# Attention of a hybrid decoder trunk in three visits to TensorE instead of five, with a bank pair lent by the dense sums

## The chip, the cores and the metric

The kernel runs on one core of one Trainium2 chip. The metric is the device time in microseconds (us) of one execution. The engines of the core work side by side, each through its own ordered queue: TensorE (PE in the profile; its weight loads are PEld), VectorE (DVE), ScalarE (ACT), GpSimdE (POOL) and SyncE (SP), which issues the weight DMAs. TensorE writes its results to PSUM, eight banks of 512 float32 per partition; VectorE and ScalarE read them from there.

## The reference

Two layers over 256 positions of width 1024, float32. Each layer is a feed-forward step, a mixing step and a second feed-forward step, each on the RMS-normalised input and added to it:

```python
def hybrid_layer(x, ...):
    x = x + 0.5 * swiglu(rms_norm(x, ffn1_norm), ffn1_w_gate_up, ffn1_w_down)
    h = rms_norm(x, mix_norm)
    z = h @ w_in                       # 512 for pooling, 3 x 512 for q, k, v, 2048 for gates
    u, q, k, v, gl = ...
    y_pool = multiscale_pool(u, pool_w, pool_scale)    # trailing means over 2/4/8/16, minus the token, a 128x128 map per group
    q = rope(rms_norm(q.reshape(B, S, 8, 64), q_norm))
    k = rope(rms_norm(k.reshape(B, S, 8, 64), k_norm))
    y_attn = moba_attention(q, k, v)
    gates = sigmoid(gl + b_gate).reshape(B, S, 2, 1024)
    merged = gates[:, :, 0] * (y_pool @ w_branch_pool) + gates[:, :, 1] * (y_attn @ w_branch_attn)
    x = x + merged @ w_out
    return x + 0.5 * swiglu(rms_norm(x, ffn2_norm), ffn2_w_gate_up, ffn2_w_down)
```

The block-sparse attention has blocks of 256 positions, and there are 256 positions: no block lies fully in the past, and what remains is plain causal attention of 8 heads of width 64.

## The kernel before

**Dense work.** Activations lie with features on partitions. Each float32 operand is split into a high and a low part (float32r). A product of a 128x128 weight block with all 256 positions is one step of `chain` (L142): the high weights with both parts of the activations (512 columns), then the low weights with the high part (256 columns). The sum of two output blocks over eight input blocks, 16 such steps, is one `sum_pair` (L173) into a tile of two PSUM banks from the pool `pmm`, which has two such tiles. `drain` (L188) evacuates it: ScalarE copies one half (L189), VectorE adds the other (L190). Only then can the pool hand these banks to the next tile.

**Weights.** `request` (L97) issues the DMA of one unit of 16 blocks (1 MB) and splits it in two halves, each by a ScalarE copy (L122) and a VectorE subtraction (L123). The split parts have six half-unit buffers, three units. Each pair of gates requests one unit while it uses an older one.

**The mixing step** (`mix`, L575) projects q, k and v by token, turns q and k to features (`to_features`), projects the pooling input (`project_u`), and then computes the eight pairs of gate columns, f = 0 to 7: `gate(f)` is one `sum_pair`, a `request` and the drain into `gates[:, f]`; `open_gate(f)` scales on VectorE (L603) and applies Tanh on ScalarE (L606). Attention and the pooling maps are laid in between, for four pairs of heads p = 0 to 3. Queries are cut at 128: the early half (positions 0 to 127) needs 128 keys, the late half 256. They use the other four PSUM banks, the pool `pat`: first as two tiles of two banks (`flat`, each holding the scores of one pair of heads, 384 columns a head), at the end as four tiles of one bank (`half_psum(4)`, `quarter`). Before the change TensorE comes to them five times in a layer:

1. in the middle of gate 0: the scores of pairs 0 and 1 (`score(0, 1)`);
2. after gate 2: the transposes of their probabilities (`turn(0, 1)`), copied to SBUF by ScalarE (`turned`, L561);
3. in the middle of gate 3: the scores of pairs 2 and 3, then the values of pairs 0 and 1 into the free quarter of the same tiles (`second`);
4. after gate 5: the transposes of pairs 2 and 3, and the pooling maps of groups 0 and 1 (`third`);
5. after gate 6: the values of pairs 2 and 3 and the maps of groups 2 and 3 (`fourth`).

`softmax` (L531) works on one pair of heads: VectorE adds the mask in PSUM (L534), takes the maxima (L538) and scales them (L540); ScalarE takes four exponentials with their sums (L543); VectorE inverts the sums (L545) and normalises (L548). `heads_end` (L661, L662) and `map_end` (L656, L657) split the results into high and low parts in `yp`. After gate 7's sum the branch products (tile `two`) read `yp`.

**Order.** Matmuls and whatever is wrapped in `keep` stay in the order written. The other instructions of ScalarE and VectorE are ordered by a planner when the program is built, which gives each engine a fixed queue; the order of VectorE and ScalarE is therefore planned anew when the code changes.

**The feed-forward step** (`ffn`, L312) opens with two pairs whose steps are interleaved. `factor_parts`, `factor_sums` and `factor_end` make the normalising factor from the sum of squares `acc`. `more` is given for a feed-forward step that follows a mixing step; without it, and without `n0`, this branch serves only the first feed-forward step of layer 1.

Of the kernel before, what the change touches and what calls it, by code (L numbers as in the profile page):

```python
# [24 lines left out]
P = 128  # L25
# [24 lines left out]
def trunk_kernel(ctx: ExitStack, tc: tile.TileContext, x_in, w_in, pw_in, qkn_in, rope_in, mask_in, band_in, out):  # L50
# [131 lines left out]
    def pair(w, t, other=None, at=0):  # L182

        ps = sum_pair(w, other, at)
        request()
        drain(t, ps)
# [125 lines left out]
    def ffn(after, n0=0, end=False, more=None):  # L312
# [18 lines left out]
        else:  # L331
# [188 lines left out]
    def scores(qT, kT, p, sc):  # L520

        for c, qs, ks in ((slice(0, S), slice(P, S), slice(0, S)), (slice(S, 3 * P), slice(0, P), slice(0, P))):
            for h in range(2):
                hs = slice(h * DH, (h + 1) * DH)
                mm(sc[:, h, c], lhsT=qT[hs, p, qs], rhs=kT[hs, p, ks], start=True, stop=True)

    COLS = (slice(S, 3 * P), slice(0, S))

    def softmax(sc, p, pr, rq):  # L531

        dg = sc[:, :, P:3 * P].rearrange("p h (a b) -> p h a b", a=2)
        tt(dg, dg, mask.unsqueeze(1).unsqueeze(1).to_broadcast([P, 2, 2, P]), op=OP.add)  # L534
        nb = small.tile([P, 2, 2], F32, name="nb", tag="nb")
        su = small.tile([P, 2, 2], F32, name="su", tag="su")
        for t, c in enumerate(COLS):
            nc.vector.tensor_reduce(nb[:, t, :], sc[:, :, c], axis=AX.X, op=OP.max)  # L538
        rp = rq.rearrange("p (t h) -> p t h", t=2)[:, :, 2 * p:2 * p + 2]
        stt(nb, nb, -1.0, rp, op0=OP.mult, op1=OP.mult)  # L540
        for h in range(2):
            for t, c in enumerate(COLS):
                act(pr[:, h, c], sc[:, h, c], AF.Exp, scale=rp[:, t, h:h + 1], bias=nb[:, t, h:h + 1],  # L543
                    accum_out=su[:, t, h:h + 1])
        nc.vector.reciprocal(su, su)  # L545
        for t, c in enumerate(COLS):
# [3 lines left out]
    def by_key(pr, pt):  # L550

        for h in range(2):
            for o, c in enumerate((2, 0, 1)):
                j = 3 * h + o
                keep(nc.tensor.transpose(line(pt)[:, j * P:(j + 1) * P], pr[:, h, c * P:(c + 1) * P], ident))  # L555

    def line(z):
        return z.rearrange("p h s -> p (h s)")

    def to_key(pt, pT):  # L560
        act(line(pT)[:, :6 * P], line(pt)[:, :6 * P], AF.Copy)  # L561

    def values(pT, v, p, y):

        for i, t in ((0, 0), (1, 0), (1, 1)):
            for s in range(2):
                h = 2 * p + s
                c = (3 * s + i + t) * P
                mm(y[s * DH:(s + 1) * DH, i], lhsT=v[:, t, h * DH:(h + 1) * DH],
                   rhs=line(pT)[:, c:c + P], start=t == 0, stop=t == i)  # L570
# [4 lines left out]
    def mix(l, after):  # L575
# [23 lines left out]
        def gate(f, *other):  # L599
            pair(unit(), gates[:, f], *other)  # L600
# [71 lines left out]
        rest = slice(3 * P, 4 * P)  # L672
# [4 lines left out]
        ats = []  # L677

        def score(*ps):
            ats[:] = [flat() for _ in ps]  # L680
            for p, sc in zip(ps, ats):
                scores(qT, kT, p, sc)

        def turn(*ps):
            ats[:] = [flat() for _ in ps]
            for p, pt in zip(ps, ats):
                by_key(pp[:, p % 2], pt)

        def turned(*ps):
            for p, pt in zip(ps, ats):  # L690
                to_key(pt, pp[:, 2 + p % 2])

        def second():
# [263 lines left out]
```

## Time and profile before

| | |
|---|---|
| median of 3 runs | 998.58 us (998.3 to 1006.34) |
| the profiled execution | 998.18 us |
| its span, first to last instruction | 996.3 us |
| TensorE busy | 991.8 us (100%) |
| VectorE busy | 812.7 us (82%) |
| ScalarE busy | 637.3 us (64%) |
| granted TensorE clock | 1.000 |
| from HBM | 190.82 MB, 193 GB/s over the span |

Times in the profile are microseconds from the first instruction of the span, unless marked ns. A row of the timeline gives start, duration, engine, line and operation, output<-inputs and, in brackets, the engine's idle time before it with what ended it. Successive instructions overlap a little at their ends, so that a row's duration is somewhat longer than the time for which it holds its engine. A row of the chain of waits gives start, length, engine, tile and line, and the number of instructions. A row of the groups gives line, engine, operation, tiles and shapes, the count, then the sum of busy time, the mean in ns and the idle time before them. A float32 matmul that is not split appears as two instructions. Layer 1's gates begin at about 720 us, layer 0's at about 227 us.

### The profile page before, as it was taken

What the parts mean: (1) busy time and instruction counts of PE and PEld (TensorE: products, weight loads), DVE (VectorE), ACT (ScalarE), POOL (GpSimd) and SP (SyncE); (2) the same over time, 40 slices, a digit from 0 to 9 for tenths busy, and PEclk for the clock granted to TensorE, in tenths of its full rate; (3) what the DMA queues carried; (4) which work ended last, traced back from release to release, by engine and by line L of the source; (5) the groups of instructions that cost most, each with busy time, mean ns of one, the idle gap of its engine ahead of it and who ended that gap; (6) DMA issues with size and microseconds to landing.
All of it is one profiled execution on the core that took longest, in us unless ns stands there. A gap on an engine that the chain in (4) does not pass through costs nothing.

```text
span 996.3 us, 15513 instructions
## 1 busy us (share of the span) xinstructions
PE 991.8 (100%) x6059; PEld 891.3 (89%) x6059; DVE 812.7 (82%) x1227; ACT 637.3 (64%) x1028; POOL 3.5 (0%) x54
## 2 busy tenths in 40 slices
PE   9999999999999999999999999999999999999998
PEld 8898889898898989888989889888989989889887
DVE  7987786699889998886678888667998999888752
ACT  7766565657867866665566666556678668656541
POOL 1000000000000000000000000000000000000000
PEclk9999999999999999999999999999999999999999
DMA  9665566653635665656555655555545356655540
GB/s 314 242 208 209 192 245 216 214 177 113 226 127 180 234 221 186 203 204 205 184 204 178 208 206 180 207 206 191 186 152 198 110 190 232 228 203 184 211 143 27
DMA packets 30152, 192.86 MB, mean 194 GB/s; under 512 B 3360, under 2 KB 5408, under 8 KB 7552
## 3 DMA queue, kind: packets, MB, share of 16 engines
q1 hardware_dynamic: 29664, 191.18, 55.1%
q8 instruction: 47, 0.77, 0.3%
q10 hardware_dynamic: 288, 0.31, 0.1%
q0 software_dynamic: 128, 0.39, 0.1%
q14 instruction: 25, 0.20, 0.1%
HBM read 190.82 MB, written 1.05 MB: 193 GB/s over the span
## 4 chain that ended last, share of the span: by engine, by line
PE 99%; DMA 0%; ACT 0%; SPq 0%; DVE 0%; issue 0%
PE ps L80 85%; PE pt L80 6%; PE two L80 4%; PE at L80 2%; PE at L555 1%; PE pe L80 0%; DMA raw<-w 0%; PE tp L516 0%; PE ss L80 0%; ACT hi L122 0%; SPq L834 0%; DVE gx L460 0%; ACT hx L252 0%
## 5 line engine op out<-in xcount | busy, mean ns | idle before, releaser
L80 PE MATMUL ps<-hx,hi 128*128 128x512 f32 (+1 forms) x1714 | 571.9, 383 | 0.1
L123 DVE TENSOR_TENSOR lo<-raw,hi 128x1024 fp32r<-128x1024 f32 (+2 forms) x333 | 392.4, 1186 | 110.5 <-ACT hi L122 106.6
L80 PE MATMUL ps<-hx,lo 128*128 128x256 f32 x1712 | 464.3, 273 | 0.0
L122 ACT ACTIVATE hi<-raw 128x1024 fp32r<-128x1024 f32 (+2 forms) x333 | 339.0, 1028 | 177.5 <-PE ps L80 148.1
L80 PEld LDWEIGHTS ps<-hx,hi 128*128 128x128 f32 x1714 | 320.8, 188 | 57.3 <-issue 0.3
L80 PEld LDWEIGHTS ps<-hx,lo 128*128 128x128 f32 x1712 | 320.9, 188 | 0.9 <-DVE lo L123 0.2
L80 PE MATMUL ps<-ga,hi 128*128 128x512 f32 x256 | 86.9, 382 | 0.0
L80 PE MATMUL ps<-gc,hi 128*128 128x512 f32 x256 | 86.9, 382 | 0.0
L80 PE MATMUL ps<-ga,lo 128*128 128x256 f32 x256 | 69.9, 273 | 0.0
L80 PE MATMUL ps<-gc,lo 128*128 128x256 f32 x256 | 69.9, 273 | 0.0
L80 PE MATMUL ps<-gb,hi 128*128 128x512 f32 (+1 forms) x197 | 65.6, 377 | 0.0
L80 PE MATMUL pt<-hi,hx 128*128 128x512 f32 x192 | 64.5, 383 | 0.0
L80 PEld LDWEIGHTS ps<-gc,hi 128*128 128x128 f32 x256 | 48.1, 188 | 8.6
L80 PEld LDWEIGHTS ps<-ga,hi 128*128 128x128 f32 x256 | 48.1, 188 | 8.6
L80 PE MATMUL pt<-lo,hx 128*128 128x256 f32 x192 | 52.5, 273 | 0.0
L80 PE MATMUL ps<-gb,lo 128*128 128x256 f32 x192 | 52.4, 273 | 0.0
L190 DVE TENSOR_TENSOR ab<-ps,ab 128x512 f32<-128x512 f32 x56 | 38.5, 688 | 16.1 <-ACT ab L189 14.8
L80 PEld LDWEIGHTS ps<-ga,lo 128*128 128x128 f32 x256 | 48.1, 188 | 0.0
L80 PEld LDWEIGHTS ps<-gc,lo 128*128 128x128 f32 x256 | 48.1, 188 | 0.0
L397 DVE TENSOR_TENSOR lo<-raw,hi 128x1024 fp32r<-128x1024 f32 x38 | 44.7, 1217 | 0.0
L80 PE MATMUL two<-yp,hi 128*128 128x512 f32 x128 | 42.8, 382 | 0.0
L80 PE MATMUL ps<-mk,hi 128*128 128x512 f32 x128 | 42.8, 382 | 0.0
(161 smaller groups left out, 1126.2 us busy)
## 6 DMA issues: line engine op xcount, KB each, us to landing
raw<-w SPq DMA_DIRECT2D x176, 1024.0 KB, 4.9
raw<-w SPq DMA_DIRECT2D x6, 256.0 KB, 6.1
raw<-w SPq DMA_DIRECT2D x11, 128.0 KB, 3.8
raw<-w SPq DMA_DIRECT2D x2, 512.0 KB, 7.3
gx<-x SPq DMA_DIRECT2D x2, 256.0 KB, 5.3
qk<-pw SPq DMA_DIRECT2D x2, 256.0 KB, 2.7
out_dram<-gx SPq DMA_DIRECT2D x2, 256.0 KB, 2.1
out_dram<-gx SPq DMA_DIRECT2D x1, 384.0 KB, 5.8
```

Of the source, the lines that this page charges most:

```text
L80: return keep(nc.tensor.matmul(*args, **kw))
L122: put(act(hi, w, AF.Copy))
L123: put(tt(lo, w, hi.bitcast(F32), op=OP.subtract))
L190: put(tt(t, ps[:, :, 0, :], t, op=OP.add))
L397: keep(tt(lo[h], raw[:, h * HALF:(h + 1) * HALF], hi[h].bitcast(F32), op=OP.subtract))
L555: keep(nc.tensor.transpose(line(pt)[:, j * P:(j + 1) * P], pr[:, h, c * P:(c + 1) * P], ident))
```

## The change

TensorE comes to attention three times in a layer.

- `score`, in the middle of gate 0: the scores of all four pairs. The late queries' scores go to the two tiles of `pat`, two pairs in each (256 columns a head). The early queries' scores of all pairs go to a tile `low` that is taken from `pmm`, the pool of the dense sums. `largest` then makes the masked early scores in SBUF (one wide add into `pp`), masks the late ones in PSUM, and takes all maxima of the layer (three reductions, one scaling). Gate 1's sum is written into the same `low` tile.
- `softmax` is left with exponentials, inverse and normalisation, one pair after each of gates 0 to 3.
- `turn`, after a quarter of gate 5's sum: all 24 transposes, the early ones into a second `low` tile from `pmm`, the late ones into two tiles of `pat`; then one ScalarE copy of the early ones and four of the late ones. Gate 6's sum is written into that second `low` tile.
- `finish`, in the middle of gate 6: all values and all four pooling maps, into four tiles of one bank, and their drains.

The matmuls themselves keep their number and their sizes. In the first feed-forward step of layer 1 the two opening pairs are interleaved in another order, the drain of the first comes ahead of the factor, the factor's sum over partitions stands before the last eight steps of the second pair instead of behind them, and three instructions lose their `keep`.

```diff
-    def sum_pair(w, other=None, at=0):
-        ps = banks(pmm, "ps")
+    def sum_pair(w, other=None, at=0, ps=None):
+        ps = ps or banks(pmm, "ps")
...
-            for u, k0, k1 in ((0, 0, 6), (1, 0, 4), (0, 6, NK)):
+            for u, k0, k1 in ((0, 0, 6), (1, 0, 4), (0, 6, NK)) if more else ((0, 0, 7), (1, 0, 2), (0, 7, NK), (1, 2, 4)):
                 columns(ws[u], pss[u], range(k0, k1))
-            ar = factor_parts(keep)
-            drain(ts[0], pss[0], keep)
-            for _ in range(1 if more else 0):
+            if more:
+                ar = factor_parts(keep)
+                drain(ts[0], pss[0], keep)
                 more()
+            else:
+                drain(ts[0], pss[0])
+                r.append(factor_end(factor_sums(factor_parts())))
             columns(ws[1], pss[1], range(4, NK))
-            r.append(factor_end(factor_sums(ar)))
+            if more:
+                r.append(factor_end(factor_sums(ar)))
...
+    def largest(ats, low, pp, rq):
+        tt(pp[:, :, :, LOW], low, mask.unsqueeze(1).unsqueeze(1).to_broadcast([P, 4, 2, P]), op=OP.add)
+        nb = small.tile([P, 2, 8], F32, name="nb", tag="nb")
+        for i, at in enumerate(ats):
+            for p in range(2):
+                dg = at[:, :, p, P:]
+                tt(dg, dg, bc2(mask), op=OP.add)
+            nc.vector.tensor_reduce(nb[:, 1, 4 * i:4 * i + 4].rearrange("p (a h) -> p a h", h=2),
+                                    at.rearrange("p h a s -> p a h s"), axis=AX.X, op=OP.max)
+        nc.vector.tensor_reduce(nb[:, 0].rearrange("p (a h) -> p a h", h=2), pp[:, :, :, LOW], axis=AX.X, op=OP.max)
+        stt(nb, nb, -1.0, rq.rearrange("p (t h) -> p t h", t=2), op0=OP.mult, op1=OP.mult)
+        return nb
...
+        def score():
+            low.append(banks(pmm, "low"))
+            lo = low[0].rearrange("p h a (b c) -> p (a b) h c", c=P)
+            for p in range(4):
+                scores(qT, kT, p, lo[:, p], slice(0, P), slice(0, P))
+            for p in range(4):
+                if p % 2 == 0:
+                    two.append(flat().rearrange("p h (a s) -> p h a s", s=S))
+                ats.append(two[-1][:, :, p % 2])
+                scores(qT, kT, p, ats[p], slice(P, S), slice(0, S))
+            nb.append(largest(two, lo, pp, rq))
+
+        def turn():
+            low.append(banks(pmm, "low"))
+            lo = low[1].rearrange("p h a (b c) -> p (a b) h c", c=P)
+            for p in range(4):
+                by_key(lo[:, p], pp[:, p], 2)
+            ats[:] = [z[:, :, p] for z in [flat().rearrange("p h (a s) -> p h a s", s=S) for _ in range(2)]
+                      for p in range(2)]
+            for p in range(4):
+                for c in range(2):
+                    by_key(ats[p][:, :, c * P:(c + 1) * P], pp[:, p], c)
+            keep(act(pp[:, :, :, :P], lo, AF.Copy))
+            for p in range(4):
+                keep(act(pp[:, p, :, P:3 * P], ats[p], AF.Copy))
+
+        def finish():
             half_psum(4)
+            ats[:] = [z[:, p, :] for z in [quarter("at") for _ in range(4)] for p in range(2)]
+            for p in range(4):
+                values(pp[:, p], v, p, by_half(ats[p]))
+            for p in range(4):
+                pool_map(p, ats[4 + p])
+            for p in range(4):
+                heads_end(p, by_half(ats[p]))
+            for p in range(4):
+                map_end(p, ats[4 + p])
...
-        gate(0, lambda: score(0, 1), NK // 2)
-        softmax(ats[0], 0, pp[:, 0], rq)
+        gate(0, score, NK // 2)
+        attend(0)
         open_gate(0)
-        gate(1)
-        softmax(ats[1], 1, pp[:, 1], rq)
+        gate(1, ps=low[0])
+        attend(1)
         open_gate(1)
         pool_diff()
         gate(2)
+        attend(2)
         open_gate(2)
-        turn(0, 1)
-        turned(0, 1)
-        gate(3, second, NK // 2)
-        for p in range(2):
-            heads_end(p, ats[p][:, :, rest])
-        softmax(ats[0], 2, pp[:, 0], rq)
+        gate(3)
+        attend(3)
         open_gate(3)
         gate(4)
-        softmax(ats[1], 3, pp[:, 1], rq)
         open_gate(4)
-        gate(5)
+        gate(5, turn, NK // 4)
         open_gate(5)
-        third()
-        turned(2, 3)
-        for p in range(2):
-            map_end(p, line(ats[p])[:, 6 * P:])
-        gate(6)
+        gate(6, finish, NK // 2, ps=low[1])
         open_gate(6)
-        fourth()
-        for p in range(2):
-            heads_end(2 + p, by_half(ats[p]))
-            map_end(2 + p, ats[2 + p])
         last = sum_pair(unit())
```

`attend(p)` calls `softmax` with the scores, probabilities and maxima of pair p; `scores` and `by_key` now write one half of a pair at a time into the place they are given.

More of the change, by code (lines that the diff above doesn't have):

```diff
@@ L180, in sum_pair, with pair @@
         return ps
-    def pair(w, t, other=None, at=0):
-        ps = sum_pair(w, other, at)
+    def pair(w, t, other=None, at=0, ps=None):
+        ps = sum_pair(w, other, at, ps)
         request()
@@ L518, in to_features, with scores @@
             act(zT[:, :, t * P:(t + 1) * P], tp[:, t], AF.Copy)
[L520 to L535, printed above, removed]
+    def scores(qT, kT, p, sc, qs, ks):
+        for h in range(2):
+            hs = slice(h * DH, (h + 1) * DH)
+            mm(sc[:, h], lhsT=qT[hs, p, qs], rhs=kT[hs, p, ks], start=True, stop=True)
@@ L536, in softmax @@
+    def softmax(at, p, pr, rq, nb):
+        rp = rq.rearrange("p (t h) -> p t h", t=2)
         su = small.tile([P, 2, 2], F32, name="su", tag="su")
[L537 to L540, printed above, removed]
         for h in range(2):
-            for t, c in enumerate(COLS):
-                act(pr[:, h, c], sc[:, h, c], AF.Exp, scale=rp[:, t, h:h + 1], bias=nb[:, t, h:h + 1],
+            n = 2 * p + h
+            for t, c, z in ((0, LOW, pr[:, h, LOW]), (1, HIGH, at[:, h])):
+                act(pr[:, h, c], z, AF.Exp, scale=rp[:, t, n:n + 1], bias=nb[:, t, n:n + 1],
@@ L544, in softmax, with by_key @@
                     accum_out=su[:, t, h:h + 1])
         nc.vector.reciprocal(su, su)
[L546 removed]
+        for t, c in enumerate((LOW, HIGH)):
             n = c.stop - c.start
             tt(pr[:, :, c], pr[:, :, c], su[:, t, :].unsqueeze(2).to_broadcast([P, 2, n]), op=OP.mult)
[L550 removed]
+    def by_key(z, pr, c):
         for h in range(2):
[L553 to L555 removed]
@@ L557, in line @@
[L557 to L561, printed above, removed]
+            keep(nc.tensor.transpose(z[:, h], pr[:, h, c * P:(c + 1) * P], ident))
     def values(pT, v, p, y):
@@ L597, in mix, with gate @@
         nc.vector.tensor_scalar(rh, rt, 0.5, None, op0=OP.mult)
-        def gate(f, *other):
-            pair(unit(), gates[:, f], *other)
+        def gate(f, *other, **kw):
+            pair(unit(), gates[:, f], *other, **kw)
         def open_gate(f):
@@ L671, in mix @@
         yk, pk = ([yp[:, i] for i in range(a, a + 4)] for a in (0, 4))
-        rest = slice(3 * P, 4 * P)
         def flat():
             return banks(pat, "at").rearrange("p h a s -> p h (a s)")
[L677 to L693, printed above, removed]
-            score(2, 3)
-            for p in range(2):
-                values(pp[:, 2 + p], v, p, ats[p][:, :, rest])
-        def third():
-            turn(2, 3)
-            for p in range(2):
-                pool_map(p, line(ats[p])[:, 6 * P:])
-        def fourth():
-            half_psum(4)
-            ya, yb = quarter("at"), quarter("at")
-            ats[:] = [z[:, p, :] for z in (ya, yb) for p in range(2)]
-            for p in range(2):
-                values(pp[:, 2 + p], v, 2 + p, by_half(ats[p]))
-            for p in range(2):
-                pool_map(2 + p, ats[2 + p])
+        ats, low, two, nb = [], [], [], []
@@ new lines, in finish, with attend @@
+        def finish():
+            half_psum(4)
+            ats[:] = [z[:, p, :] for z in [quarter("at") for _ in range(4)] for p in range(2)]
[7 more added lines that the diff above has]
+                map_end(p, ats[4 + p])
+        def attend(p):
+            softmax(ats[p], p, pp[:, p], rq, nb[0])
```

7 lines of the change are left out of this document (2 added, 5 removed).

## The prediction

> **What bounds the kernel now.** I read the page's span, busy table and chain of waits first, then the chain in order of time around the attention of layer 1 (layer 0 is the same 493 us earlier), then VectorE and ScalarE by themselves in that stretch.
>
> ```profile
> span 996.3 us, 15513 instructions
> ...
> PE 991.8 (100%) x6059; PEld 891.3 (89%) x6059; DVE 812.7 (82%) x1227; ACT 637.3 (64%) x1028; POOL 3.5 (0%) x54
> ...
> PE 99%; DMA 0%; ACT 0%; SPq 0%; DVE 0%; issue 0%
> ```
>
> 99% of the chain is TensorE. Only two things can move the end: TensorE's own work, and a wait put into its strictly ordered stream. There is next to no idle time on it to take away. In order of time (start, length, what, matmul instructions):
>
> ```profile
> 720.38 2.74 PE ps L80 x16
> 723.12 1.51 PE at L80 x16
> 724.62 13.54 PE ps L80 x80
> 738.16 1.31 PE at L555 x12
> 739.47 2.67 PE ps L80 x16
> 742.14 2.97 PE at L80 x40
> 745.11 13.55 PE ps L80 x80
> 758.66 1.31 PE at L555 x12
> 759.97 0.68 PE at L80 x6
> 760.65 5.34 PE ps L80 x32
> 765.99 2.37 PE at L80 x30
> 768.36 5.35 PE ps L80 x32
> 773.70 21.33 PE two L80 x128
> ```
>
> `ps` is dense work: 16 instructions (a high and a low pass for each of 8 blocks) take 2.67, so a gate's sum is 5.34. `at` is attention: scores (1.51), transposes (1.31 for two pairs of heads), scores with values (2.97), transposes with two maps, values with two maps. No row is a wait. What lies beside it, in the 32 us from the first gate:
>
> ```profile
> 720.00:752.00 32.00, 32.00 (x225) 28.39 (x224) 31.61 (x59) 24.41 (x54) 0.00 (x0) 1.00 0.45 165
> ```
>
> The columns are length, then TensorE, weight loads, VectorE 31.61, ScalarE 24.41, GpSimd; then granted clock 1.00. VectorE is full here. The weights don't suffer: they are prepared three units ahead. But whatever VectorE must deliver on a date is at risk.
>
> **TensorE's work.** The change keeps every matmul: 16 score products, 24 transposes, 24 value products and 12 map products a layer, in the same sizes. What falls is the number of entries into these odd shapes:
>
> ```profile
> 722.62 0.38 PE L80 MATMUL ps<-hx,hi 128*128 128x512 f32 x1
> 722.84 0.27 PE L80 MATMUL ps<-hx,lo 128*128 128x256 f32 x1
> 723.05 1.58 PE L80 MATMUL at<-qk 64*128 64x256 f32 x16
> ```
>
> Between dense matmuls a high one holds 0.22 (722.62 to 722.84), so a low one holds 0.11 (2.67/8 = 0.33 less 0.22); the low one ahead of the scores holds 0.21. Entry costs 0.10. The dense stretch behind a visit is 13.54 where five times 2.67 make 13.35: the return costs 0.19 (13.55 behind the values: 0.20). Transposes cost neither (2.67 and 5.34 behind them). Before: scores twice, values twice, with entries from dense work at 723, 742 and 766, one turn from scores to values inside the 2.97, and returns at 724.6 and 745.1; the last visit goes out through full-size maps. After: scores once, values once, the values again leaving through maps. So one entry (0.10), the turn from scores to values (as an entry, 0.10) and one return (0.20) go: 0.4, and with the slow first pair of a visit, which these rows bound at nothing to 0.2, I take 0.5 a layer, 1.0 in all. This is the change's whole gain.
>
> **The borrowed bank pair.** TensorE's sums rotate over two pairs of banks (`pmm`, two buffers). Twice a layer the change takes one as `low` in the middle of a sum, when the other holds the sum itself. So the previous sum must be drained by then, no longer a whole gate later. What does a drain take? These are VectorE's closing adds of gates 0 to 6:
>
> ```profile
> 730.52 0.68 DVE L190 TENSOR_TENSOR gates<-ps,gates 128x512 f32<-128x512 f32 x1
> ...
> 735.08 0.68 DVE L190 TENSOR_TENSOR gates<-ps,gates 128x512 f32<-128x512 f32 x1
> ...
> 741.49 0.68 DVE L190 TENSOR_TENSOR gates<-ps,gates 128x512 f32<-128x512 f32 x1
> ...
> 751.21 0.68 DVE L190 TENSOR_TENSOR gates<-ps,gates 128x512 f32<-128x512 f32 x1
> ...
> 755.46 0.68 DVE L190 TENSOR_TENSOR gates<-ps,gates 128x512 f32<-128x512 f32 x1
> ...
> 761.80 0.68 DVE L190 TENSOR_TENSOR gates<-ps,gates 128x512 f32<-128x512 f32 x1
> ...
> 768.21 0.68 DVE L190 TENSOR_TENSOR gates<-ps,gates 128x512 f32<-128x512 f32 x1
> ```
>
> By the chain the sums end at 727.49 (724.62 + 0.20 + 2.67), 732.82, 738.16, 747.99, 753.32, 758.66 and 765.99. The adds end 3.7, 2.9, 4.0, 3.9, 2.8, 3.8 and 2.9 later: mean 3.44. Hidden today under the next sum's 5.34. With both engines free it is much less:
>
> ```profile
> 714.20 0.60 ACT L189 ACTIVATE uT<-ps 128x512 f32<-128x512 f32 x1 [3.13 <-PE ps L80]
> ```
>
> ```profile
> 714.83 0.69 DVE L190 TENSOR_TENSOR uT<-ps,uT 128x512 f32<-128x512 f32 x1 [1.50 <-ACT uT L189]
> ...
> 721.71 0.68 DVE L190 TENSOR_TENSOR uT<-ps,uT 128x512 f32<-128x512 f32 x1
> ```
>
> ScalarE starts when the sum ends, 714.20, and the add is over at 715.52: 1.32.
>
> First loan, amid gate 0: the pair wanted is that of `project_u`'s second sum, whose add ends at 722.39; the scores begin at 723.05. It fits, by 0.66.
>
> Second loan, `turn` amid gate 5: it comes after a quarter of the sum, 1.33 after gate 4's end. Gate 4's pair is the one wanted, since gate 5's sum sits in the other. Drain 1.32 at best, 3.44 as measured: TensorE waits 0.0 to 2.7 (4.0 - 1.33), and I take 3.44 - 1.33 = 2.1 a layer, because at this place VectorE is as full as where the seven were taken. All 24 transposes, 12 of gate 5's blocks and everything after queue behind it; VectorE and ScalarE use the pause, so nothing else grows, but TensorE gets none of it back.
>
> The same `turn` also waits for all four softmaxes. Today the last ends here, 1.9 ahead of its transposes (758.66):
>
> ```profile
> 756.06 0.68 DVE L548 TENSOR_TENSOR pp<-pp,su 128x512 f32<-128x512 f32 x1
> ```
>
> ```profile
> L538 DVE TENSOR_REDUCE nb<-at 128x2 f32<-128x256 f32 (+1 forms) x16 | 8.1, 549 | 0.0
> ...
> L534 DVE TENSOR_TENSOR at<-at,mask 128x512 f32<-128x512 f32 x8 | 5.5, 692 | 0.1
> ...
> L493 DVE TENSOR_REDUCE ms<-rows 128x16 f32<-128x1024 f32 x4 | 4.8, 1211 | 0.0
> ...
> L502 DVE TENSOR_TENSOR k<-k,ri 128x1024 f32<-128x1024 f32 x2 | 2.4, 1220 | 0.0
> ```
>
> After, the date is 720.38 + 31.1 = 751.5 (gate 0's start, five and a quarter sums of 5.34, 3.0 of scores). Masks and maxima cost a layer 4 x 0.69 + 8 x 0.55 = 7.1 today; in `largest` one wide add (as L502, 1.22), four adds of half today's columns (between half of 0.69 and 0.69) and three reductions of 1024 (1.21): 6.2 to 7.6. No saving that counts, and all in one lump on a VectorE that is full, with maxima of all pairs due before the first exponential. So softmax and drain come late together; they overlap as one wait, not two. If VectorE puts both weight splits of gate 4's request (two wide subtractions, each as L502's 1.22) ahead of the drain, the wait becomes 4.5.
>
> **Waits with cover.** Gate 1 starts on `low` after one wide add, 1.22, under eight high-score instruction pairs and half a sum (over 4). Gate 6 starts on the second `low` after one ScalarE copy under 12 blocks (4.0). The value products wait for five copies, which move what these four of 0.82 move (3.3), under 12 blocks of gate 5 and 8 of gate 6 (6.7). The branch products wait for all eight drains of `finish`, today the last at 771.64:
>
> ```profile
> L561 ACT ACTIVATE pp<-at 128x768 f32<-128x768 f32 x8 | 6.1, 824 | 0.0
> ```
>
> ```profile
> 771.16 0.48 DVE L657 SCALAR_TENSOR_TENSOR yp<-at,hb,yp 128x256 fp32r<-128x256 f32 x1 [0.61 <-ACT yp L656]
> ```
>
> ```profile
> 499.01 0.38 PE L80 MATMUL ps<-hx,hi 128*128 128x512 f32 x1
> ```
>
> ```profile
> 504.04 0.48 DVE L253 SCALAR_TENSOR_TENSOR hx<-gx,hx 128x256 fp32r<-128x256 f32 x1
> ...
> 505.34 0.43 DVE L206 TENSOR_TENSOR ar<-acc,ar 128x256 fp32r<-128x256 f32 x1 [0.48 <-ACT ar L205]
> ```
>
> That is 2.06 early; with twice as many drains and 2.67 more cover I take nothing, at worst 1. The DMA issues on SP keep their order and are paced by freed weight buffers. In layer 1's first feed-forward which begins at 499.01, the last feature, ready at 504.52, is now wanted after 18 blocks (6.0, at 505.0), and the factor's sum after 24 (8.0, at 507.0) with its operand ready at 505.77: nothing, at worst 0.5 once.
>
> **Sum.** Profiled execution 998.18, of which 996.3 is span; the median of three is 998.58. 998.18 - 1.0 + 2 x 2.1 = 1001.4.
>
> **Rivals.** (a) *No wait at all*: gate 4's drain is done in 1.3 and the softmaxes in time. Then 998.2 - 1.0 = 997.2, and to the median 997.6. For it: VectorE's order is planned anew, and weight splits can be put off. Against: none of seven drains came under 2.8. 0.20. (b) *VectorE's lump*: drains of gates 2 and 3, splits and softmaxes queue behind `largest` and the pooling differences, so that starts of gates 4 and 5 wait too; 4.5 (2.1 and two subtractions) to 5 a layer and more, at 4.75 998.2 - 1.0 + 9.5 = 1006.7. It decides once more than 2.4 of put-off splits stand ahead of the drain. For: 31.61 of 32.00. Against: the splits' lead. 0.15, of which 0.06 lies beyond a per cent. (c) *The clock*: wait and 24 transposes in a row make 2.1 + 2.6 = 4.7 without a dense matmul. Today's twelve in a row, 1.31, leave the clock at 1.00 in the row above, and no gap of 4.7 is in the trace. If the clock fell to half afterwards for as long as the gap, it would cost 2.35 a layer: 1001.4 + 4.7 = 1006.1. 0.08, as nothing in the trace shows it. The Trainium skill, TensorE: Matmul & The Clock Gate, Part 1 and Part 4, has the clock halved after an idle window of about 3.4 us and says that transposes don't count as activity; by it the loss would be 1.7 a layer, estimated 1004.8. No run here shows either. (d) The forecast, waits of 0.8 to 3.3 a layer: 998.8 to 1003.8. 0.55. The rest, 0.02, is a surprise.
>
> **The numbers.** 1001.4. From (a) to most of (b) and (c): 996.9 (the best case less another 0.3 for the entries that the rows bound) to 1006.3. About 1% is what counts as a difference. Faster by that is nearly excluded, as TensorE's work can't fall by 10: 0.01. Slower, beyond 1008.6, needs waits of 5.7 a layer: 0.06 from (b) and 0.02 from (c) or beyond. Within: 0.91.
>
> **What would show it.** A row of waiting ahead of the first transposes of gate 5, ended by VectorE's add into `gates`, of 1 to 3; two dense stretches fewer followed by 0.2. Wrong if that wait is missing, if gates 4 or 5 start late, or if the granted clock dips.

## The result, and the profile after

The changed kernel took 1006.72 us in the median of nine runs (1005.59 to 1010.41), the kernel before 998.51 beside it: a ratio of 1.0075, 95% interval 1.0054 to 1.0096. It is slower, by less than the one per cent that counts as a difference. The forecast was 1001.4, in a range up to 1006.3: the median lies 0.4 above the range. Some executions of one kernel are longer than the others for a reason that no trace shows (of 90 of the kernel before, 74 took 998.1 to 999.3 and 16 took 1002.5 to 1007.0; e10 below took 998.7 to 998.9 in six and 1002.8 to 1003.2 in six; e5 took 1000.3 when it was profiled and 1002.0 to 1002.5 in its other nine), so the stages of the profiled executions are what is compared below, and a median means little without its interval.

The page of the changed kernel (1007.07 us, of which 1005.2 is span): the span, the busy table and the engines' shares of the chain that ended last.

```profile
span 1005.2 us, 15491 instructions
...
PE 994.0 (99%) x6059; PEld 892.3 (89%) x6059; DVE 813.7 (81%) x1213; ACT 639.0 (64%) x1030; POOL 3.7 (0%) x54
...
PE 90%; DVE 4%; ACT 2%; DMA 2%; issue 0%; SPq 0%; ACTq 0%
```

The work of no engine has changed by more than 2.2 us, but TensorE fell from 99% of the chain to 90%. Where the rest went is seen in the chain in order of time, around layer 1's attention (start, length, what; the scores begin at 728.43):

```profile
719.89 4.90 PE ps L80 x29
...
724.86 1.07 ACT hi L122
725.94 0.02 issue
725.96 1.23 DVE lo L123
...
728.55 1.02 DVE gates L635
...
736.83 1.14 DVE nb L540
...
748.19 1.50 ACT pp L553 x6
...
750.49 1.99 ACT hi L122 x2
...
758.87 1.22 DVE lo L123
760.09 0.61 DVE gates L190
760.70 0.04 issue
760.75 1.09 PE low L563 x8
```

From 724.8 to 760.7 the chain has no TensorE in it. It runs over VectorE and ScalarE: pooling additions (L635), maxima (`nb`), exponentials (`pp` L553), weight splits (`hi`, `lo`), and the drain (L190) for which the borrowed banks wait. Before the change the same stretch was TensorE throughout. The view of TensorE's waits between 740 and 765 names three (total, times, longest):

```profile
PE ps L80 <- ACT hi L122: 1.4, 1, 1.4
PE low L563 <- DVE gates L190: 1.2, 1, 1.2
PE ps L80 <- DVE lo L123: 0.8, 1, 0.8
```

By the distances between the starts of successive matmuls these cost 1.56, 1.35 and 1.04. The second is the predicted one, at the transposes. The other two stand at the start of gate 4: its weights are not split. Why they are late is in ScalarE's timeline (the bracket is idle time and what ended it):

```profile
734.11 1.06 ACT L122 ACTIVATE hi<-raw 128x1024 fp32r<-128x1024 f32 x1 [4.63 <-PE ps L80]
...
738.68 0.49 ACT L553 ACTIVATE pp<-pp,nb,ri 128x128 f32<-128x128 f32 x1 [1.72 <-DVE nb L543]
...
750.49 1.99 ACT L122 ACTIVATE hi<-raw 128x1024 fp32r<-128x1024 f32 x2
```

and in VectorE's:

```profile
728.55 1.01 DVE L635 TENSOR_TENSOR gates<-uT 128x813 f32<-128x813 f32 x1
...
729.93 0.71 DVE L635 TENSOR_TENSOR gates<-gates 128x538 f32<-128x538 f32 x1
730.56 1.22 DVE L123 TENSOR_TENSOR lo<-raw,hi 128x1024 fp32r<-128x1024 f32 x1
731.70 1.22 DVE L534 TENSOR_TENSOR pp<-low,mask 128x1024 f32<-128x1024 f32 x1
...
738.48 0.16 DVE L543 SCALAR_TENSOR_TENSOR nb<-nb,ri 128x16 f32<-128x16 f32 x1
...
751.56 2.36 DVE L123 TENSOR_TENSOR lo<-raw,hi 128x1024 fp32r<-128x1024 f32 x2 [0.53 <-ACT hi L122]
...
760.01 0.68 DVE L190 TENSOR_TENSOR gates<-ps,gates 128x512 f32<-128x512 f32 x1
```

VectorE begins the lump of maxima 3.3 us after the scores begin, behind pooling additions and a split, and scales them at 738.48, done 10.2 us after the scores. (Before, the first pair's maxima were ready after 4.7.) ScalarE idles 4.63 and 1.72 us meanwhile (the first until TensorE gives back a weight buffer for the split at 734.11, the second until the maxima come), and afterwards has the exponentials of three pairs ahead of the split that gate 4 needs at 750.0. It starts that split at 750.49. Neither data nor a buffer held it back: by the order of the issues these weights had landed at 722.55, and a buffer was free from about 736.9, when TensorE went on to gate 1's second half. It starts some 25 us after gate 0 begins; before the change it started after some 16.

In layer 0 the granted clock fell as well, just after gate 4's waits. A table by stretch (length; busy TensorE, weight loads, VectorE, ScalarE, GpSimd; granted clock, share of DMA, GB/s):

```profile
249.84:253.25 3.41, 2.92 (x18) 2.38 (x16) 3.01 (x7) 3.41 (x12) 0.00 (x0) 1.00 0.00 0
253.25:256.67 3.42, 1.75 (x9) 1.34 (x10) 2.89 (x4) 3.42 (x8) 0.00 (x0) 1.00 0.00 0
256.67:260.08 3.41, 3.41 (x13) 2.93 (x12) 3.34 (x6) 3.41 (x8) 0.00 (x0) 0.50 0.76 243
260.08:263.49 3.41, 3.41 (x21) 3.05 (x21) 2.79 (x4) 2.17 (x4) 0.00 (x0) 1.00 0.42 115
```

For 3.41 us TensorE ran at half speed: 13 matmuls where the next stretch has 21.

The 8.9 us of span add up by stages. Let the mixing stage be the time from the first transpose of `q` to the first branch product. It took 65.74 in both layers before; it takes 69.81 and 69.30. That is 7.6. Another 1.4 stand before layer 0's mixing stage, in the start-up, where the first factor's sum came at 29.7 instead of 28.4; in the experiments it came at 28.2 to 29.1, so it is put down to chance; of the three other executions of the changed kernel with the same mean clock, 0.998, two took 1005.59 and 1005.61, 1.5 less than the profiled one. The rest of layer 0 and the first feed-forward of layer 1 went from 427.71 to 427.62. Within layer 1: 1.56 + 1.04 + 1.35 of waits less 3.56 leaves 0.39 that the merged visits saved. In layer 0, waits of 1.56, 1.04 and 0.24, less 0.39, leave 1.6 of the 4.07 for the fall of the clock. Both the 0.39 and the 1.6 are remainders of such sums. The account holds for the profiled execution: two of the nine, the median one among them, have a mean clock of 1.000, thus no such fall, and what they spend instead can't be told without a trace.

### The profile page after: what moved, and what is told of

The parts are those of the page before. It is cut to its first block, busy times and chain, and to the rows that moved or that the text cites. A ratio compares the mean times of both kernels' runs of the same rounds, so it can differ in the third digit from the quotient of the medians.

```text
span 1005.2 us, 15491 instructions
## 1 busy us (share of the span) xinstructions
PE 994.0 (99%) x6059; PEld 892.3 (89%) x6059; DVE 813.7 (81%) x1213; ACT 639.0 (64%) x1030; POOL 3.7 (0%) x54
## 3 DMA queue, kind: packets, MB, share of 16 engines
HBM read 190.82 MB, written 1.05 MB: 191 GB/s over the span
## 4 chain that ended last, share of the span: by engine, by line
PE 90%; DVE 4%; ACT 2%; DMA 2%; issue 0%; SPq 0%; ACTq 0%
PE ps L80 77%; PE pt L80 6%; PE two L80 4%; DMA raw<-w 1%; DVE lo L123 1%; PE low L80 1%; ACT hi L122 1%; PE at L80 1%; ACT pp L553 1%; DVE nb L540 0%; DVE gates L635 0%; DVE gates L190 0%; DMA gx<-x 0%; PE at L563 0%; ACT gates L607 0%
## 5 line engine op out<-in xcount | busy, mean ns | idle before, releaser
L80 PE MATMUL ps<-hx,hi 128*128 128x512 f32 (+1 forms) x1650 | 552.2, 384 | 3.6 <-ACT hi L122 3.0
L80 PE MATMUL ps<-hx,lo 128*128 128x256 f32 x1648 | 447.9, 274 | 1.9 <-DVE lo L123 1.9
L80 PEld LDWEIGHTS ps<-hx,hi 128*128 128x128 f32 x1650 | 309.4, 188 | 59.5 <-ACT hi L122 3.8
L80 PEld LDWEIGHTS ps<-hx,lo 128*128 128x128 f32 x1648 | 309.7, 188 | 3.7 <-DVE lo L123 2.8
L190 DVE TENSOR_TENSOR ab<-ps,ab 128x512 f32<-128x512 f32 x56 | 38.5, 688 | 15.5 <-ACT ab L189 14.2
```

What stands on the lines that cost most here:

```text
L80: return keep(nc.tensor.matmul(*args, **kw))
L190: put(tt(t, ps[:, :, 0, :], t, op=OP.add))
```

## The experiments

The theory after the result: the maxima come in one lump and late, so ScalarE first idles and then has its exponentials ahead of gate 4's splits; the wait at the transposes is separate. Rivals: the order in ScalarE's queue by itself; VectorE's amount of work; transposes letting the clock fall. Line numbers shift by a few in the experiments (the exponentials are L556, the transposes L566, the pooling additions L634 and L640, the remainder of the pooling L641 to L646). All waits are per layer (layer 0 / layer 1), by distances of starts as above; the maxima's time is counted from the start of the scores. A fall of the clock is a stretch at a granted clock of 0.50; the one that every trace has at its very end isn't counted.

| kernel | median us | ratio to before, 95% interval | mixing stage us | maxima ready us | wait at gate 4 us | wait at transposes us | falls of the clock |
|---|---|---|---|---|---|---|---|
| before | 998.51 | | 65.74 / 65.74 | 4.7 (first pair) | 0 | 0 | 0 |
| after | 1006.72 | 1.0075 [1.0054, 1.0096] | 69.81 / 69.30 | 10.2 | 2.60 / 2.59 | 0.24 / 1.35 | 1 |
| e1 | 1004.29 | 1.0049 [1.0031, 1.0066] | 69.30 / 69.54 | 10.2 | 2.58 / 2.58 | 0 | 2 |
| e2 | 1009.27 | 1.0095 [1.0064, 1.0125] | 71.96 / 70.22 | 10.0 | 1.93 / 1.93 | 2.48 / 2.49 | 1 |
| e3 | 1008.83 | 1.0090 [1.0055, 1.0125] | 69.44 / 71.05 | 7.6 and 9.7 | 1.05 / 1.04 | 2.78 / 2.66 | 1 |
| e4 | 1001.45 | 1.0027 [1.0010, 1.0045] | 66.99 / 66.92 | 7.6 and 9.8 | 1.07 / 1.06 | 0.1 | 0 |
| e5 | 1002.16 | 1.0027 [1.0015, 1.0039] | 66.92 / 66.92 | 6.6 and 9.0 | 0.56 / 0.54 | 0.57 / 0.34 | 0 |
| e6 | 1015.80 | 1.0161 [1.0131, 1.0192] | 74.53 / 74.28 | 9.7 | 0.71 / 0.86 (and 5.1 at gate 1) | 0 | 2 |
| e8 | 1007.46 | 1.0085 [1.0059, 1.0111] | 70.47 / 70.45 | 12.3 | 0 (2.3 at gate 2) | 0.76 / 1.09 | 2 |
| e9 | 1006.50 | 1.0065 [1.0043, 1.0088] | 70.62 / 69.75 | 9.9 and 12.7 | 0 (2.4 at gate 2) | 0 | 2 |
| e10 | 1000.84 | 1.0013 [0.9996, 1.0030] | 66.04 / 66.06 | 5.6 (first pair) | 0 | 0 | 0 |
| e11 | 1001.28 | 1.0014 [0.9998, 1.0030] | 66.86 / 66.85 | 7.1 and 9.5 | 0.51 / 0.50 | 1.01 / 0.78 | 0 |
| e12 | 1001.62 | 1.0033 [1.0021, 1.0046] | 66.73 / 66.72 | 5.6 and 8.0 | 0 | 1.46 / 1.43 | 0 |

### e1: the transposes later

```diff
-        gate(5, turn, NK // 4)
+        gate(5, turn, 3 * NK // 4)
```

> The changed kernel with the transposes after three quarters of gate 5's sum instead of one quarter. If the wait ahead of them (0.24 in layer 0, 1.35 in layer 1) is the drain of the lent bank pair, it goes, since 4.0 us now lie between gate 4's end and the loan, and nothing else moves: 1 to 2 us less than the changed kernel, about 1005, with the 2.6 us at gate 4's start still there in both layers. If it is the softmaxes that are late, some wait stays. If my forecast had been right in its place (the loan is the main loss), the time would come back to about 999.

The wait for the borrowed banks is gone in both layers. TensorE's waits that are left (layer 1):

```profile
PE ps L80 <- ACT hi L122: 1.4, 1, 1.4
PE ps L80 <- DVE lo L123: 0.8, 1, 0.8
```

Both belong to gate 4, unchanged, and now the clock falls in both layers. So the loan was the smaller part: most of the loss is gate 4's weights and what follows from them.

### e2: pooling behind the maxima (inconclusive)

```diff
-                tt(sums[:, i, :], src[:, 0, PAD:], src[:, 0, PAD - h:W - h], op=OP.add)
+                first = tt(sums[:, i, :], src[:, 0, PAD:], src[:, 0, PAD - h:W - h], op=OP.add)
+                if i == 0:
+                    keep(first)
...
             nb.append(largest(two, lo, pp, rq))
+            pool_diff()
...
         open_gate(1)
-        pool_diff()
         gate(2)
```

> The changed kernel with the pooling differences pinned behind the maxima on VectorE. Theory of the late start: ScalarE stands idle for 6 us because all maxima come in one lump mixed with pooling work, and its exponentials then push the weight splits of gate 4 back. Then the maxima come 2 to 4 us sooner, the 2.6 us at gate 4's start shrink below 0.7 in each layer, and the time is 999 to 1002. Rival, too much work in too short a stretch: ScalarE has the same exponentials before the same date, gate 4 waits 2 us or more and the time stays near 1006.

The edit held only one small addition behind the maxima. The second chain of additions (L640 in later kernels), which doesn't depend on it, ran ahead as before, and the maxima came after 10.0 us instead of 10.2. It tested nothing of what it was meant to. It shows one thing all the same: in a new order with about the same lateness, the wait at the transposes was 2.5.

### e3: two sets of maxima

The maxima of pairs 0 and 1 are finished and scaled before those of pairs 2 and 3, in a tile of their own.

```diff
+        nbs = []
         for i, at in enumerate(ats):
+            nb = small.tile([P, 2, 4], F32, name="nb", tag="nb")
...
-        nc.vector.tensor_reduce(nb[:, 0].rearrange("p (a h) -> p a h", h=2), pp[:, :, :, LOW], axis=AX.X, op=OP.max)
-        stt(nb, nb, -1.0, rq.rearrange("p (t h) -> p t h", t=2), op0=OP.mult, op1=OP.mult)
+            nc.vector.tensor_reduce(nb[:, 0].rearrange("p (a h) -> p a h", h=2),
+                                    pp[:, 2 * i:2 * i + 2, :, LOW], axis=AX.X, op=OP.max)
+            stt(nb, nb, -1.0, rq.rearrange("p (t h) -> p t h", t=2)[:, :, 4 * i:4 * i + 4], op0=OP.mult, op1=OP.mult)
+            nbs.append(nb)
```

> The changed kernel with the maxima of pairs 0 and 1 finished and scaled before those of pairs 2 and 3 are begun. Late start: the first exponentials begin about 2.5 us sooner, ScalarE's idle time shrinks by as much, gate 4's wait falls by 2 us or more a layer; 1000 to 1003. Too much work: no change beyond 1 us.

The first maxima came 2.6 us earlier and the wait at gate 4 fell from 2.6 to 1.05, with the same work: it hangs on when the maxima come. The wait for the banks then grew to 2.7, so the kernel as a whole was no better.

### e4: the three together

The edits of e1, e2 and e3.

> All three edits together. Late start with the drain wait: no wait of TensorE in either layer, and what the merged visits save (0.4 a layer) becomes visible: 997 to 999. Too much work: a wait of 1 us or more stays at gate 4 or at the transposes, 1001 or more. The start of the kernel, 1.4 us later in the changed kernel's profile with the same order of work, should show the value of before in some of these profiles if it is chance.

Some 5 us of the 8 come back, the clock doesn't fall, and one large wait is left, for VectorE's half of gate 4's split:

```profile
PE ps L80 <- DVE lo L123: 0.9, 1, 0.9
```

### e5: the pooling truly behind the maxima

As e4, with the second chain of additions held too (`keep(second)` for its first member).

> The changed kernel with e4's three edits, and now both chains of the pooling differences are held behind the maxima on VectorE, which e2 did not achieve. Theory (the maxima come late, and everything on ScalarE with them): the first half of the maxima is ready some 5.4 us after the scores begin, where e4 had 7.6; ScalarE has its splits for gate 4 done in time, the 1.07 that is left at gate 4's start in e4 goes too, and the time is 997.5 to 998.5, at or below the kernel before. Rival (the lump is work, not order: VectorE has 31.6 of 32 us taken, and what is put off here is late elsewhere): a wait of 1 us or more a layer stays at gate 4 or appears at gate 5, 6 or at the map products, and the time is 1000.5 or more.

The first maxima came at 6.6, not at the 5.4 expected, and gate 4's weights were in time, by 0.2. But three waits of 0.2 to 0.6 for drains by VectorE took the place of one, and the stage has the length of e4 to within 0.1. The rival said that what is put off here is late elsewhere, and that is what happened.

### e6: splits ahead of exponentials

The late turn of e1, and in gates 0 to 3 the order of writing held:

```diff
-        request()
-        drain(t, ps)
+        request((), put)
+        drain(t, ps, put)
...
+                if h == t == 0:
+                    keep(e)
...
-            pair(unit(), gates[:, f], *other, **kw)
+            pair(unit(), gates[:, f], *other, put=keep if f < 4 else lambda i: i, **kw)
```

> The changed kernel with only the late turn of e1, and in gates 0 to 3 the weight splits and the drain written ahead of that gate's exponentials hold that order on ScalarE and VectorE. The maxima stay one lump, ready about 10 us after the scores begin. Theory (gate 4's weights are late because three pairs' exponentials stand ahead of their split in ScalarE's queue): the 1.54 and 1.04 that e1 still waits at gate 4's start go, the clock stays at 1.00, and the time is 998 to 999.5 against e1's 1004.3; the softmaxes end later and, if they are then late for the transposes, a wait appears there instead. Rival (VectorE is what is late: its own half of the split, or the buffers): at least 1 us stays at gate 4's start, and the time is 1001 or more.

Slower than every other version of the change, by a wait in a new place. TensorE's waits in layer 1:

```profile
PE low L80 <- DVE lo L123: 4.9, 1, 4.9
PE ps L80 <- DVE lo L123: 0.7, 1, 0.7
```

and VectorE's timeline there:

```profile
741.49 0.18 DVE L543 SCALAR_TENSOR_TENSOR nb<-nb,ri 128x16 f32<-128x16 f32 x1
741.58 2.36 DVE L123 TENSOR_TENSOR lo<-raw,hi 128x1024 fp32r<-128x1024 f32 x2
```

In the order of writing gate 0's request is for gate 1's weights, and held there it stands behind the maxima. The lead of three units is thus not in the code. The planner makes it, by drawing splits forward as far as the buffers allow, and it gives the lead away as freely. Neither theory had this; the question it was to answer (ScalarE's order by itself) stays unanswered by it.

### e7: 72 transposes in a row, without the change

```diff
-                keep(nc.tensor.transpose(line(pt)[:, j * P:(j + 1) * P], pr[:, h, c * P:(c + 1) * P], ident))
+                for _ in range(6):
+                    keep(nc.tensor.transpose(line(pt)[:, j * P:(j + 1) * P], pr[:, h, c * P:(c + 1) * P], ident))
```

> The kernel before, with each transpose of the probabilities issued six times into the same place: 72 in a row, where 12 took 1.31 us, at two places of each layer, so about 7.8 us in a row without a dense matmul. It measures by itself whether transposes hold the clock up. If they do, the granted clock stays at 1.00 and the time is that of the added work: 4 x 60 x 0.109 = 26 us more, 1024.7. If they do not, the records show the clock at 0.50 at the end of each of the four rows of transposes or right behind them, for 3.4 us at least, the later transposes take twice their time, and the time is 1031 or more (1.7 us for each fall, and up to 4 us a place for the transposes that run at half clock).

It took 1024.63 us in its one execution, where 1024.7 was expected if transposes hold the clock up. The stretch of 72 transposes in layer 1, and the one behind it (columns as above):

```profile
751.36:759.38 8.02, 8.02 (x75) 8.02 (x74) 7.05 (x8) 5.76 (x9) 0.00 (x0) 1.00 0.67 250
759.38:763.00 3.62, 3.62 (x28) 3.08 (x29) 0.00 (x0) 1.77 (x2) 0.00 (x0) 1.00 0.84 306
```

Eight us with next to nothing but transposes, more than twice 3.4, and the clock stays at 1.00. The Trainium skill, TensorE: Matmul & The Clock Gate, Part 4, says that the transpose mode doesn't count as the engine being busy in the same way; these float32 transposes kept the clock up. (The trace lists them as matmuls with the identity, and doesn't tell whether they run in the mode that the page means.) So transposes in a row are not what made the clock fall in the other kernels; every fall there lies at or right behind a wait.

### e8, e9 and e10: the pooling sums on GpSimd

e8 is the changed kernel with this edit alone, e9 adds the late turn and the two sets of maxima, e10 is the kernel before with it.

```diff
-                tt(sums[:, i, :], src[:, 0, PAD:], src[:, 0, PAD - h:W - h], op=OP.add)
+                nc.gpsimd.tensor_tensor(sums[:, i, :], src[:, 0, PAD:], src[:, 0, PAD - h:W - h], op=OP.add)
...
-                    tt(dst[:, :, lo:], src[:, 1:, lo:], src[:, 1:, lo - h:W - h], op=OP.add)
+                    nc.gpsimd.tensor_tensor(dst[:, :, lo:], src[:, 1:, lo:], src[:, 1:, lo - h:W - h], op=OP.add)
```

> The changed kernel, and nothing else but the seven additions of the pooling sums of each layer (four of 0.42 us, one each of 1.01, 0.71 and 0.43 on VectorE: 3.8 us a layer) given to GpSimd, which has nothing to do there. Theory (VectorE is full when the lump of maxima arrives, and what it is late with makes ScalarE late): the maxima are ready about 7 to 8 us after the scores begin instead of 10.2, the 2.6 us at gate 4's start shrink to under 1, no fall of the clock comes from there, and the time is 1000 to 1003. Rival (the lump by itself, or ScalarE's order, is enough): the maxima may come earlier but at least 2 us stay at gate 4, 1005 or more. A third case: GpSimd and VectorE slow each other, so that VectorE's additions of the same size take visibly longer than 0.42 and 0.68 us, and nothing is won.

> The late turn of e1 and the two sets of maxima of e3, with the pooling sums on GpSimd as in e8. Theory (what is left in e4 and e5 is VectorE's work, 1.1 to 1.2 us a layer whichever instruction is late): all waits go, the mixing stage takes 65.3 to 65.5 us a layer instead of 65.74 before the change (the 0.4 that the merged visits save), and the time is 997.4 to 998.0, below the kernel before. Rival (the order of ScalarE and the borrowed pair cost by themselves): a wait of 0.5 us or more stays in each layer, 999.0 or more.

> The kernel before with the pooling sums on GpSimd and nothing else: what that edit is worth without the change. Before the change no row of TensorE waits, so all theories expect 998.3 to 998.7, no difference; if GpSimd and VectorE slow each other, or the planner's order suffers, waits appear and it is over 999.

e8 and e9 came out against the theory, for a reason that it had not seen. VectorE's timeline in e8:

```profile
734.50 0.23 DVE L638 TENSOR_TENSOR gates<-gates,inv 128x64 f32<-128x64 f32 x1 [2.50 <-POOL gates L631]
734.64 1.21 DVE L542 TENSOR_REDUCE nb<-pp 128x8 f32<-128x1024 f32 x1
```

A small operation that reads GpSimd's sums was queued ahead of the maxima, and VectorE stood still for 2.50 us before it. The maxima came after 12.3, and the drain behind them made gate 2 wait 2.3. Once more what costs is the place in a fixed queue. By its interval e10 can't be told from the kernel before; its profile shows one wait of 0.35 a layer, at the value products, and a mixing stage longer by 0.3.

### e11: GpSimd's sums, read behind the maxima

e9, with `pool_diff()` called directly after `largest` and its first reading operation held there:

```diff
-            tt(e, sums[:, :, :PAD], inv, op=OP.mult)
+            keep(tt(e, sums[:, :, :PAD], inv, op=OP.mult))
```

> e9 with one thing mended: in e8 and e9 VectorE's fixed queue held the first operation that reads GpSimd's pooling sums ahead of the maxima, and waited 2.50 us there for GpSimd; here that operation and all pooling work behind it come after the maxima. Theory (what is left in e4 and e5, 1.1 to 1.2 us a layer, is VectorE's work, of which 3.8 us a layer are now elsewhere): the first maxima are ready some 6.6 us after the scores begin as in e5, ScalarE's exponentials and splits follow, no wait of more than 0.2 us is left at gates 2 to 5 or at the transposes, the mixing stage takes 65.3 to 65.6 us against 65.74 before the change and 66.92 in e4 and e5, and the time is 997.4 to 998.2. Rival (the three visits cost that much whatever VectorE has to do): 0.8 us or more of waiting stays in each layer, with the time at 1000 or more.

The seven additions are off VectorE, 3.8 us a layer if their durations are added up; its busy time over the span falls by less, from 812.1 in e5 to 808.4, 1.9 a layer, since successive rows overlap and its subtractions beside GpSimd took longer (last section). The stage is shorter by 0.07. The amount of work is not what decides: VectorE idles 2.1 of the first 22 us after the scores, and the waits stay. The chain in order of time shows what does:

```profile
721.98 2.64 PE ps L80 x15
724.62 0.02 issue
724.64 1.06 ACT hi L122
725.70 0.02 issue
725.73 1.70 DVE lo L123
727.43 1.15 DVE pp L534
...
746.08 0.61 DVE gates L190
746.69 0.04 issue
746.74 2.71 PE ps L80 x15
```

A weight split, whose product gate 3 doesn't read until 740.9, stands ahead of the maxima on both engines, and everything to gate 4's start follows from it without a gap.

### e12: that subtraction behind the maxima

e11, with VectorE's half of the first split in gate 2's request held behind the maxima, and the rest of the pooling behind it.

```diff
-            split(raw[:, h * HALF:(h + 1) * HALF], hi[h], lo[h], put)
+            split(raw[:, h * HALF:(h + 1) * HALF], hi[h], lo[h], put, (not h and low) or put)
...
-        put(tt(lo, w, hi.bitcast(F32), op=OP.subtract))
+        low(tt(lo, w, hi.bitcast(F32), op=OP.subtract))
...
-        request()
+        request(low=low)
...
-            pair(unit(), gates[:, f], *other, **kw)
+            pair(unit(), gates[:, f], *other, low=keep if f == 2 else None, **kw)
...
-            pool_diff()
...
         gate(2)
+        pool_diff()
```

> e11 with two more places held in VectorE's queue: the subtraction of a weight split that e11's chain shows ahead of the maxima (1.70 us, its weights not used until 15 us later) comes behind them, and the rest of the pooling differences behind that. Matmuls, sizes and engines as in e11. Theory (the waits are one unbroken chain from the scores through maxima, exponentials, splits and drains, so it must begin earlier, whichever engine carries it): the first maxima are ready 5.4 us after the scores begin instead of 7.1, and both waits of e11 (0.50 at gate 4, 0.78 to 1.01 at the transposes, in series on that chain) go; at most 0.2 us a layer is left; the mixing stage takes 65.3 to 65.7 us, and the time is 997.5 to 998.3, level with the kernel before or a little below. Rival (it is the amount of work on ScalarE and VectorE in 30 us, and what is put off comes late elsewhere): 0.8 us or more of waiting stays in each layer, now at the subtraction put off (gate 3) or at the map products, and the time is 1000 or more.

The first maxima came after 5.6 us, and the waits at gates 1 to 4 are gone in both layers: this half of the theory holds. The wait at the transposes didn't go:

```profile
PE low L566 <- DVE gates L190: 1.3, 1, 1.3
```

VectorE's timeline ahead of that drain:

```profile
752.79 0.68 DVE L607 TENSOR_TENSOR gates<-gates,r 128x512 f32<-128x512 f32 x1
753.39 3.49 DVE L123 TENSOR_TENSOR lo<-raw,hi 128x1024 fp32r<-128x1024 f32 x3
756.80 0.68 DVE L190 TENSOR_TENSOR gates<-ps,gates 128x512 f32<-128x512 f32 x1
```

Three subtractions of weight splits stand ahead of the drain that lends the banks. By the uses of their weights the first was needed within 0.2 us, the second after 5.8, the third after 11.7. An order with the last two (2.3 us) behind the drain was not tried, so that the change would then be free of waits is argued, not shown. The new order also cost 0.5 to 0.7 us at the second feed-forward of each layer (the rest went from 427.62 to 428.54).

With one wait left, the saving is read best here: 65.74 + 1.43 - 66.72 = 0.45 a layer. No version beat the kernel before.

## Why the prediction was right and wrong

**Right: the class, and the gain.** Within one per cent, on the slow side. For the class that was partly luck: the sum had 4.2 of waits, all at the transposes, and of the 8.9 that came, 5.2 at gate 4, 1.6 of clock and 1.4 of start-up were in no term of it. By the prediction's own signs of being wrong, two came true: gate 4 started late, and the granted clock dipped. The merged visits were put at 0.5 a layer from entries and returns of 0.1 and 0.2; 0.39 was measured in the changed kernel and 0.45 in e12. The feed-forward's new order was put at nothing: 0.09 less. The first loan fitted by 0.66 by the sum, and there is no wait ahead of the scores. `largest` was put at 6.2 to 7.6 us: 1.22 + four masks of 0.4 + three reductions of 1.21 are 6.5.

**Right in its mechanism: the second loan.** The transposes wait for VectorE's drain of gate 4, as forecast, with 2.1 a layer. In the changed kernel it was 0.24 and 1.35, since TensorE came later by gate 4's waits; in e2 and e3, with the same turn, 2.5 to 2.8; with the turn 2.67 later still 1.4 in e12. The sentence on splits queued ahead of the drain is what the rows show.

**Wrong: "The weights don't suffer: they are prepared three units ahead."** This step failed, and with it "the splits' lead" that spoke against rival (b). Gate 4's weights were 2.6 us late in each layer, 5.2 of the 8.9. The lead is the planner's doing and not the code's (e6), and one lump of maxima used it up. It can be counted, from the end of VectorE's half of a split to TensorE's first product with it: before the change it was 6 to 15 us in layer 1, shortest at gate 3; in the changed kernel it is 13.1 for the first half of gate 3, 6.5 for the second, and 0.06 for the first of gate 4, which TensorE stood waiting for. The premise was in the text ("maxima of all pairs due before the first exponential"), but its price was sought on VectorE alone, as softmaxes that end late. They didn't matter; the last probabilities were ready 4 us ahead of the transposes. What was not asked is what ScalarE does until the maxima come (in the first 22 us after the scores it idles 7.5 us, 3.8 before), and what then stands behind its exponentials. e3 shows the link: 2.6 us earlier maxima take 1.5 off the wait. In e12, which has e11's work in another order and the first maxima at 5.6, it is gone. How much of the 2.6 is ScalarE's order alone stays open, as e6 did not test it.

**Rival (b) was nearest**: starts of gates late as well, 1006.7. Its place was close (gate 4, not 4 and 5), but its ground, that VectorE is full, is not borne out. Taking the seven additions off VectorE (e11) moved the stage by 0.07; it is the order in two fixed queues that decides. That its time is the measured one is luck: it had 9.5 of waits, and there were 6.8, with the clock and the start-up making up the rest.

**Rival (c), the clock**, came true as an event and not as told. In the changed kernel the clock fell once, at gate 4's weights and not at the transposes, and cost 1.6 in layer 0. In e2 and e3, with waits of 2.5 and 2.7 at the transposes, it fell there once each. The estimate of 1.7 by the Trainium skill (TensorE: Matmul & The Clock Gate, Part 1) has the right size. Its premise about transposes didn't hold for those of e7.

The sum, then: 1.4 of start-up, 5.2 at gate 4, 1.6 at the transposes, 1.6 of clock, less 0.8 for the visits and 0.1 for the feed-forward, is 8.9.

## What to carry to other kernels

When small pieces of work are gathered into one lump, ask of every engine that reads the result what it does until the lump is done and what is then queued behind it, not only whether the engine that makes the lump has the time. A lead that a planner makes is no reserve: look in the trace at who produces the lead, and count how late its producer may start. A wait that moves from place to place as edits are made (here gate 4, the transposes, gate 2, gate 1) is the sign of one chain over fixed queues; follow it back to where it starts before removing its ends.

## What the runs showed of the hardware that was not expected

**The clock falls after a stretch that is only about half idle.** All falls lasted 3413 ns, or twice that after the single wait of 5.1 us in e6. Within a run they lie whole multiples apart: 146.0 in e1 (253.38 and 751.73), 147.0 in e6 (239.47 and 741.23). So there is a fixed grid. The Trainium skill, TensorE: Matmul & The Clock Gate, Part 1, describes such a free-running window of 3413 ns, and says that the clock falls after an idle one. Here it fell after windows in which TensorE was busy for a good part. In e1, layer 1 (columns as above):

```profile
748.32:751.73 3.41, 1.52 (x7) 1.14 (x8) 2.88 (x4) 3.41 (x8) 0.00 (x0) 1.00 0.00 0
751.73:755.14 3.41, 3.41 (x13) 2.83 (x12) 3.34 (x7) 3.41 (x10) 0.00 (x0) 0.50 0.66 214
```

Over all kernels, windows at full clock that were busy for 1.66 us or less, and the one of the changed kernel with 1.75, were followed by a fall; those busy for 1.79 or more never were. One in e3 with 1.68, much of it transposes, was not either, so the bound is not exact. In e6 the windows after the falls, at half clock and busy for 2.18 and 1.78, were followed by a second window at half clock. Two waits of together 2.6 us are enough if they fall into one window, and the same waits that straddle two (layer 1 of the changed kernel) cost nothing more. The number of falls also seems to change from one execution of a kernel to the next: in e1 the mean clock is 1.000, 0.998 or 0.997, which fits none, one and two falls of 3.4 us (the profiled execution has 0.997 and two), and the shortest times with these are 1002.99, 1003.97 and 1005.17, some 1.0 to 1.2 us a fall.

**GpSimd and VectorE slowed each other, but only in some pairings.** An addition of 256 columns took 0.42 on VectorE and 0.61 on GpSimd, one of 813 columns 1.01 and 1.54. In e8 to e12 all 18 of VectorE's subtractions of 1024 columns that ran beside a GpSimd addition took 1.60 to 1.70 (one is the row of e11's chain above) instead of 1.22, and in e8 to e11 the second GpSimd addition of 256 columns, beside such a subtraction, took 1.47. In e12, where that subtraction was put off, the same addition ran beside VectorE's masking add (L534), which reads PSUM: it took 0.61, and the masking add its usual 1.22.
